# Partial sums kept in the token order of a head group, and another order of work in the first pair of a seven-product projection

## The chip, the cores and the metric

The kernel runs on one core of one Trainium2 chip. The metric is the device time of one execution in microseconds (us). Three executions of the kernel before took 2134.4, 2132.32 and 2133.94 us, so the median is 2133.94 us. One more execution was profiled: it took 2131.81 us, with a span of 2130.1 us from its first to its last instruction.

The engines are named as in the profile: PE is TensorE (matrix products), PEld its weight loads, DVE is VectorE, ACT is ScalarE, POOL is GpSimd, SP is SyncE, which here issues most of the transfers.

## The reference, cut to what matters

Two layers run over 1024 tokens of 1024 channels. The first mixes tokens with a gated position mixer, the second with dilated attention; each is followed by a dense squared-ReLU block. The change lies in the projection in front of the attention:

```python
WINDOW_DILATIONS = ((128, 1), (512, 4), (2048, 16))     # head groups g = 0, 1, 2
qkv = (h @ w_qkv).reshape(B_, S_, 3, N_DIL_GROUPS, ATT_HEADS, HEAD_DIM)
...
# in group g, query t attends to keys t - j*dilation, j = 0 .. window//dilation
s = einsum('bnqrhc,bnkrhc->bnrhqk', qb, kc) * HEAD_DIM ** -0.5
p = exp(logits - m); den = sum(p); num = einsum('bnrhqk,bnkrhc->bnqrhc', p, vc)
```

With dilation 4 or 16 the tokens that attend to each other are 4 or 16 apart. The kernel therefore keeps Q, K and V of group 1 and group 2 in another token order: all tokens of residue 0 first, then residue 1, and so on (`r q` in the code), while a projection comes out of PE in plain token order (`q r`). Group 0 has plain order in both.

## The kernel before, in words

**Units and pairs.** The attention is cut into 12 units, one for each pair of heads `hp` (4) and head group `g`, taken in the order of groups 1, 2, 0. Unit 0 is (hp 0, group 1), unit 1 is (hp 0, group 2), unit 2 is (hp 0, group 0), unit 3 is (hp 1, group 1), and so on. Each unit needs three tiles of 128 output channels by 1024 tokens: m = 0 is Q, m = 1 is K, m = 2 is V. The 36 tiles are projected two at a time. The first four tiles (Q, K and V of unit 0, and Q of unit 1) are done by the plain method (`classical`); the other 32 are 16 pairs, listed in `quads`. The pairs are made by `seven` (L1207 ff.).

**Seven products in place of eight.** A pair is a 2x2 block product (two tiles by two halves of 512 tokens). `one(p)` issues one of seven products: 4 blocks of 3 matmuls each, 12 matmuls of 128x512, into a bank of PSUM. There are three such banks (`mm`). `copied` (L1219, ACT) moves one product from PSUM to SBUF, `plus` (L1225, DVE) adds another product to a sum in SBUF, and `put_out` makes the four finished blocks: block (i, s) is tile i of the pair, token half s. Between products `more()` splits the weights of the next pair into a high and a low part (L205 on ACT, L206 on DVE), after some subtractions on POOL (L410 to L415).

**Where the order of tokens is changed.** `out_v` (V, L1144) and `out_qk` (Q and K, L1189) add the last product to the sum and write the result in the group's order. The inputs are read in plain order and the output is written with a stride. For Q and K ACT then writes the high part (L1192) and DVE the low part (L1193). A V block is transposed on PE and split (L1132 on ACT, L1133 on DVE). A block that is a single product has no addition: ACT (L1142 for V, L1192 for Q and K) and DVE (L1193) read it straight from PSUM, in the group's order.

**The attention beside it.** `attention` is a generator that is advanced between products. For each unit there are four rounds j: `scores` (PE matmuls into the `at` banks, then DVE adds the bias and takes a minimum, L1288, and ACT takes the exponential, L1290), `turned` (PE transposes, L187; ACT and DVE split the result, L205 and L206 with the tile name `tr`) and `values` (PE matmuls of `tr` with V; ACT copies the sum, L1327). The place of each step on PE is set by a count of PE time that the program keeps while it is written down (`Flow`): a step is put after the product at which its due time has passed. PE keeps exactly this order; on the other engines a scheduler decides the order when the program is built.

One rule cuts across this. When the first block of a K tile is put out, the program first runs the attention until all four score rounds of the unit before it are on PE:

```python
if m == 1 and i > 0:
    flow.until(lambda: U[i - 1].scored.t is not None)
u.tiles[m] = [slot((P, S), F32R, f"{'qk'[m]}{e}") for e in range(2)]
```

What `flow.until` has to bring forward stands on PE without products in between.

**The first pair.** For the first pair (`first=True`) the order of products is 1, 3, 6, 2, 7, 5, 4, since the terms for the products 4 and 5 are formed last. Tile 0 of this pair is K of unit 1, tile 1 is V of unit 1. The first block that is put out is (0, 0), after product 2.

Of the kernel before, what the change touches and what calls it, by code (L numbers as in the profile page):

```python
# [112 lines left out]
def trunk(ctx: ExitStack, tc: tile.TileContext, xT, w_u, w_v, w_o, w_s, b_s, w_qkv, w_bo, rel,  # L113
# [14 lines left out]
    def temp():  # L128
        return tpool.tile([P, HALF], F32, tag="t", name="t", bufs=NT)
# [950 lines left out]
    def permuted(t, s, g):  # L1080
# [4 lines left out]
        n = HALF // d  # L1085
        return t.rearrange("p (r q) -> p q r", r=d)[:, s * n:(s + 1) * n, :]

    def runs(t, g):
        return t if g == 0 else t.rearrange("p (q r) -> p r q", r=DIL[g])

# [7 lines left out]
    def own(t, g):  # L1098
        return t if g == 0 else t.rearrange("p (q r) -> p q r", r=DIL[g])
# [39 lines left out]
    def put(dst, a, b):  # L1139

        if b is None:
            nc.scalar.activation(dst, a, AF.Copy)  # L1142
        else:
            nc.vector.tensor_tensor(dst, a, b, op=ALU.add)  # L1144

    def out_v(i, s, a, b):

        u = U[i]
        ready = []
        with tc.high_priority(offset=PRIO):  # L1150
            if u.g < 2:
                t = temp()
                if u.g == 1 and b is None:
                    put(t.rearrange("p (r q) -> p r q", r=4), runs(a, 1), None)
                else:
                    put(t if u.g == 0 else t.rearrange("p (r q) -> p q r", r=4), own(a, u.g),
                        None if b is None else own(b, u.g))
                ready.append((s, t))
            else:
                for e in range(2):  # L1160
                    if e not in u.vt:
                        u.vt[e] = temp()
                    c = slice(8 * e, 8 * e + 8)
                    if b is None:
                        put(u.vt[e].rearrange("p (r q) -> p r q", r=8)[:, :, 32 * s:32 * s + 32], runs(a, 2)[:, c, :], None)
                    else:
                        put(u.vt[e].rearrange("p (r q) -> p q r", r=8)[:, 32 * s:32 * s + 32, :], own(a, 2)[:, :, c],
                            own(b, 2)[:, :, c])
                u.out += 1
                if u.out == 2:  # L1170
                    ready = [(e, u.vt.pop(e)) for e in range(2)]
        for part, t in ready:
            flow.add(v_side(i, t, part), LAT["ve"] + (500 if b is None else 1500) + (5000 if i == 0 else 0))

    def out_qk(i, m, s, a, b, over):

        u = U[i]
        if m not in u.tiles:
# [3 lines that stand above are left out]
        hi, lo = (runs_at(t, s, u.g) for t in u.tiles[m])  # L1182
        sc = -0.125 if m == 0 else 1.0
        with tc.high_priority(offset=PRIO):
            if b is None:
                a = runs(a, u.g)
            else:
                t = a if over and u.g == 0 else temp()
                nc.vector.tensor_tensor(t if u.g == 0 else t.rearrange("p (r q) -> p q r", r=DIL[u.g]),  # L1189
                                        own(a, u.g), own(b, u.g), op=ALU.add)  # L1190
                a = t if u.g == 0 else t.rearrange("p (r q) -> p r q", r=DIL[u.g])
            nc.scalar.activation(hi, a, AF.Copy, scale=sc)  # L1192
            nc.vector.scalar_tensor_tensor(lo, a, sc, hi.bitcast(F32), op0=ALU.mult, op1=ALU.subtract)  # L1193
        u.out_qk = getattr(u, "out_qk", 0) + 1
        if u.out_qk == 4:
            u.q, u.k = u.tiles[0], u.tiles[1]
            u.qk.t = flow.t

    def out(tile, s, a, b=None, over=False):

        i, m = tile
        if m == 2:
            out_v(i, s, a, b)
        else:
            out_qk(i, m, s, a, b, over)

    def seven(w, x, more, put_out, begun=None, first=False):  # L1207

        def one(p, bank=None):
            new = bank is None  # L1210
            bank = mm_bank() if new else bank
            product(bank, w[p], x.t[p], p in (2, 3, 4) and not (first and p == 3))
            more()
            return bank

        def copied(src):
            t = temp()
            with tc.high_priority(offset=PRIO):
                nc.scalar.activation(t, src, AF.Copy)  # L1219
            return t  # L1220

        def plus(x, y, out=None):
            out = temp() if out is None else out
            with tc.high_priority(offset=PRIO):
                nc.vector.tensor_tensor(out, x, y, op=ALU.add)  # L1225
            return out

        if first:
            a = one(1)
            u = copied(a)  # L1230
            d = one(3)
            plus(u, one(6), u)
            one(2, a)
            put_out(0, 0, a)
            e = one(7)
            c22 = plus(u, e)
            f = one(5)
            put_out(1, 1, c22, f, True)
            put_out(0, 1, plus(u, f), d, True)
        else:  # L1240
            u = one(6)
            if begun:
                begun()
            u = copied(u)
            a = one(1)
            plus(u, a, u)
            d = one(5)
            c22 = plus(u, d)
            e = one(7)
            put_out(1, 1, c22, e, True)  # L1250
            one(2, a)
            put_out(0, 0, a)
            one(3, d)
            put_out(0, 1, u, d)
        one(4, e)
        put_out(1, 0, u, e, True)

    def geometry(g, j):

# [265 lines left out]
    def ahead_of_last():  # L1525

        N = [slot(name="N") for _ in range(3)]
        for hp in range(3):
            nc.sync.dma_start(N[hp], kept_N[hp])
        yield 4000  # L1530
        for hp in range(3):
            for i in range(2):
                split_N(hp, i, N[hp][:, half(i)])
                yield 900
            proj_load(hp)
            yield 900
        proj_load(3)
        for k in range(KT):
            h[k] = slot(name=f"h{k}")
            nc.sync.dma_start(h[k], hd[k])  # L1540

    quads = [((1, 1), (1, 2))]
    for i in range(2, NU, 2):
        quads += [((i, 1), (i, 0)), ((i, 2), (i + 1, 0)), ((i + 1, 1), (i + 1, 2))]

# [17 lines left out]
    for n, two in enumerate(quads):  # L1563
        wn = Weights(qkv(*quads[n + 1])) if n + 1 < len(quads) else None
        more = ahead(wn)
        more()
        for i, m in two:
            if m == 1:
                U[i].bias = bias_tile(U[i].hp, U[i].g)
        seven(w, xa, more, lambda i, *x: out(two[i], *x), None if wn else lambda: flow.add(ahead_of_last()), n == 0)  # L1570
        w = wn
    half_done.t = flow.t

# [114 lines left out]
```

## Time and profile before

| What | Value |
|---|---|
| Time, median of 3 | 2133.94 us (2132.32 to 2134.4) |
| Profiled execution: its time, its span | 2131.81 us, 2130.1 us |
| PE busy | 2100.7 us, 99% of the span |
| DVE busy | 1598.3 us, 75% |
| ACT busy | 1102.5 us, 52% |
| POOL busy | 556.8 us, 26% |
| Granted TensorE clock | 0.998 of full speed |
| `plus` in the attention stage (L1225) | 31 times between 1000 and 1430 us, 685 ns each |
| Last addition of Q and K (L1189) | 31 times, 677 to 1131 ns, 938 ns in the mean |
| Last addition of V (L1144) | 128x512 forms: 11 times, 862 ns; 128x256 forms: 12 times, 632 ns |

The 16 pairs stand between 975 and 1425 us of the span, and the attention runs in the same stretch. A busy share is an average over the whole kernel. To see what a local change can be worth, read where PE itself stops: PE's timeline gives the start of each run of equal instructions and their count, so the stretch between two starts, less what the same instructions take where nothing holds them, is time in which PE waited.

### The profile page before, as it was taken

What the parts mean: (1) busy time and instruction counts of PE and PEld (TensorE: products, weight loads), DVE (VectorE), ACT (ScalarE), POOL (GpSimd) and SP (SyncE); (2) the same over time, 40 slices, a digit from 0 to 9 for tenths busy, and PEclk for the clock granted to TensorE, in tenths of its full rate; (3) what the DMA queues carried; (4) which work ended last, traced back from release to release, by engine and by line L of the source; (5) the groups of instructions that cost most, each with busy time, mean ns of one, the idle gap of its engine ahead of it and who ended that gap; (6) DMA issues with size and microseconds to landing.
All of it is one profiled execution on the core that took longest, in us unless ns stands there. A gap on an engine that the chain in (4) does not pass through costs nothing.

```text
span 2130.1 us, 30439 instructions
## 1 busy us (share of the span) xinstructions
PE 2100.7 (99%) x10426; PEld 1740.4 (82%) x10426; DVE 1598.3 (75%) x2918; ACT 1102.5 (52%) x2262; POOL 556.8 (26%) x417
## 2 busy tenths in 40 slices
PE   8999999999999999999999999999999999999998
PEld 7888887888878888887888788887888887888887
DVE  7975258576689888888776867778876667988886
ACT  7644136554574444346665656665555556544443
POOL 2100213223323322531212122101133332332345
PEclk9999999999999999999999999999999999999999
DMA  6411114455354444311112121141155544544432
GB/s 223 144 60 50 40 42 137 159 182 191 128 180 165 161 145 134 113 79 52 46 46 54 34 57 41 47 160 54 60 178 180 191 149 139 186 163 140 140 107 80
DMA packets 158815, 247.07 MB, mean 116 GB/s; under 512 B 33481, under 2 KB 47940, under 8 KB 158660
## 3 DMA queue, kind: packets, MB, share of 16 engines
q1 hardware_dynamic: 158336, 244.94, 35.1%
q8 instruction: 82, 1.34, 0.3%
q14 instruction: 73, 0.60, 0.1%
q10 hardware_dynamic: 324, 0.18, 0.0%
HBM read 180.41 MB, written 64.66 MB: 115 GB/s over the span
## 4 chain that ended last, share of the span: by engine, by line
PE 89%; DVE 6%; ACT 2%; issue 1%; DMA 1%; SPq 0%; DVEq 0%; ACTq 0%
PE at L180 44%; PE mm L180 43%; PE at L187 2%; DVE wp L206 1%; DMA t<-hid 1%; DVE t L206 1%; ACT t L1290 1%; DVE h L340 0%; DVE h L940 0%; ACT wp L205 0%; SPq L169 0%; DVE hx L206 0%; DVE raws L498 0%; DVE y L206 0%; DMA h<-hd 0%
## 5 line engine op out<-in xcount | busy, mean ns | idle before, releaser
L205 ACT ACTIVATE wp<-r 128x512 fp32r<-128x512 f32 (+3 forms) x490 | 294.9, 606 | 462.6 <-PE at L180 287.4
L180 PE MATMUL at<-hx,wp 128*128 128x512 f32 x1770 | 413.8, 389 | 5.0 <-DVE wp L206 3.2
L206 DVE TENSOR_TENSOR wp<-r,wp 128x512 fp32r<-128x512 f32 (+3 forms) x490 | 374.3, 768 | 36.9 <-ACT wp L205 33.2
L180 PE MATMUL mm<-y,wp 128*128 128x512 f32 x1608 | 396.5, 392 | 1.1 <-ACT t L1219 0.5
L180 PEld LDWEIGHTS at<-hx,wp 128*128 128x128 f32 x1770 | 331.8, 188 | 76.3 <-DVE wp L206 4.1
L180 PEld LDWEIGHTS mm<-y,wp 128*128 128x128 f32 x1608 | 298.5, 188 | 65.9 <-DVE h L340 1.6
L180 PE MATMUL at<-t,wp 128*128 128x512 f32 x1344 | 314.0, 389 | 0.1
L180 PEld LDWEIGHTS at<-t,wp 128*128 128x128 f32 x1344 | 252.2, 188 | 52.8 <-DVE t L803 0.5
L410 POOL TENSOR_TENSOR t<-r 128x512 f32<-128x512 f32 (+3 forms) x78 | 111.4, 1428 | 678.1 <-DMA r<-in_w_dn 270.4
L412 POOL TENSOR_TENSOR r<-r 128x512 f32<-128x512 f32 (+3 forms) x77 | 111.8, 1452 | 377.8 <-DVE wp L206 345.1
L180 PE MATMUL mm<-t,wp 128*128 128x512 f32 x768 | 191.5, 396 | 0.0
L206 DVE TENSOR_TENSOR hx<-t,hx 128x512 fp32r<-128x512 f32 x192 | 181.5, 958 | 5.4 <-ACT hx L205 5.3
L180 PE MATMUL mm<-hx,wp 128*128 128x512 f32 x708 | 171.8, 389 | 0.0
L180 PEld LDWEIGHTS mm<-t,wp 128*128 128x128 f32 x768 | 140.5, 188 | 29.6 <-DVE t L1225 0.3
L269 POOL TENSOR_TENSOR t<-t 128x512 f32<-128x512 f32 (+1 forms) x54 | 71.7, 1328 | 347.5 <-ACT t L258 345.6
L180 PE MATMUL mm<-y,whi 128*128 128x512 f32 x512 | 158.3, 390 | 0.0
L180 PEld LDWEIGHTS mm<-hx,wp 128*128 128x128 f32 x708 | 132.7, 188 | 28.0 <-DVE b L966 0.5
L940 DVE TENSOR_TENSOR h<-h,at 128x512 f32<-128x512 f32 x144 | 97.8, 681 | 55.3 <-PE at L180 55.3
L803 DVE TENSOR_TENSOR t<-t,at 128x512 f32<-128x512 f32 x116 | 79.2, 684 | 78.1 <-PE at L180 77.9
L180 PE MATMUL at<-y,wp 128*128 128x512 f32 x552 | 137.5, 390 | 0.0
L205 ACT ACTIVATE hx<-t 128x512 fp32r<-128x512 f32 x192 | 118.0, 628 | 30.2 <-DMA t<-hid 26.2
L415 POOL TENSOR_TENSOR r<-r 128x512 f32<-128x512 f32 (+3 forms) x77 | 105.3, 1367 | 85.6 <-issue 52.7
(224 smaller groups left out, 3120.7 us busy)
## 6 DMA issues: line engine op xcount, KB each, us to landing
t<-hid SPq DMA_DIRECT2D x194, 256.0 KB, 5.0
hid<-t SPq DMA_DIRECT2D x140, 256.0 KB, 2.3
r<-in_w_up SPq DMA_DIRECT2D x128, 256.0 KB, 2.8
r<-in_w_dn SPq DMA_DIRECT2D x88, 256.0 KB, 2.7
r<-in_w_qkv SPq DMA_DIRECT2D x72, 256.0 KB, 2.7
hid<-b SPq DMA_DIRECT2D x56, 256.0 KB, 2.8
r<-in_w_v SPq DMA_DIRECT2D x48, 256.0 KB, 3.5
h<-in_xT SPq DMA_DIRECT2D x16, 256.0 KB, 3.0
```

Of the source, the lines that this page charges most:

```text
L180: nc.tensor.matmul(out, lhsT, rhs, **kw)
L187: nc.tensor.transpose(out, src, ident)
L205: nc.scalar.activation(hi, src, AF.Copy)
L206: nc.vector.tensor_tensor(lo, src, hi.bitcast(F32), op=ALU.subtract)
L269: nc.gpsimd.tensor_tensor(self.acc, self.acc, sq, op=ALU.add)
L410: tt(r7, r[0, 0], r[1, 0], op=ALU.subtract)
L412: tt(r6, r[1, 0], r[0, 0], op=ALU.subtract)
L415: tt(r3, r[0, 1], r6, op=ALU.subtract)
L803: nc.vector.tensor_tensor(out, x, y, op=ALU.add)
L940: engine.tensor_tensor(hs[i, s], hs[i, s], src, op=ALU.add)
L1290: nc.scalar.activation(p[:, c], p[:, c], AF.Exp, bias=m, scale=-1.0, accum_out=dn)
```

## The change

Four things are changed, and nothing in the arithmetic.

1. `order_of` gives each pair a token order: that of its head group, where both tiles have the same group; where one tile has group 0, the order of the second tile's group; else plain order.
2. `copied` and `plus` keep the partial sums in this order. They read the product in PSUM with a stride (`runs`) and write SBUF without one.
3. In `out_v` and `out_qk`, where the tile's group is the pair's, the last addition is made the same way: the sum is read as it is stored, the product in PSUM with a stride, and the output is written without one. Where a tile of group 0 stands in a pair of another order, its V is put back into plain order by a strided read. Where the pair has plain order and the tile another (two pairs), it stays as before.
4. In the first pair V of unit 1 is tile 0 and K of unit 1 is tile 1. Block (1, 1), K's second half, is no longer put out after product 5. The sum for it is finished in place (`plus(c22, f, c22)`) and is put out after product 4, behind block (1, 0).

```diff
+    def order_of(two):
+        a, b = (U[i].g for i, _ in two)
+        return b if a == b or 0 in (a, b) else 0
+    def stored(t, g):
+        return t if g == 0 else t.rearrange("p (r q) -> p r q", r=DIL[g])
+    def unrolled(t, g):
+        return t.rearrange("p (q r) -> p q r", r=DIL[g])
...
     def out_v(i, s, a, b, go):
...
-                if u.g == 1 and b is None:
-                    put(t.rearrange("p (r q) -> p r q", r=4), runs(a, 1), None)
+                if b is None:
+                    put(stored(t, u.g), runs(a, u.g), None)
+                elif go == u.g:
+                    put(stored(t, go), stored(a, go), runs(b, go))
+                elif u.g == 0:
+                    put(unrolled(t, go), a.rearrange("p (r q) -> p q r", r=DIL[go]), unrolled(b, go))
                 else:
-                    put(t if u.g == 0 else t.rearrange("p (r q) -> p q r", r=4), own(a, u.g),
-                        None if b is None else own(b, u.g))
+                    put(t.rearrange("p (r q) -> p q r", r=4), own(a, u.g), own(b, u.g))
...
     def out_qk(i, m, s, a, b, over, go):
...
             if b is None:
-                a = runs(a, u.g)
+                a = stored(a, go) if over else runs(a, u.g)
             else:
-                t = a if over and u.g == 0 else temp()
-                nc.vector.tensor_tensor(t if u.g == 0 else t.rearrange("p (r q) -> p q r", r=DIL[u.g]),
-                                        own(a, u.g), own(b, u.g), op=ALU.add)
-                a = t if u.g == 0 else t.rearrange("p (r q) -> p r q", r=DIL[u.g])
+                t = a if over and u.g == go else temp()
+                if u.g == go:
+                    nc.vector.tensor_tensor(stored(t, go), stored(a, go), runs(b, go), op=ALU.add)
+                else:
+                    nc.vector.tensor_tensor(t.rearrange("p (r q) -> p q r", r=DIL[u.g]), own(a, u.g), own(b, u.g), op=ALU.add)
+                a = stored(t, u.g)
...
         def copied(src):
...
-                nc.scalar.activation(t, src, AF.Copy)
+                nc.scalar.activation(stored(t, go), runs(src, go), AF.Copy)
...
         def plus(x, y, out=None):
...
-                nc.vector.tensor_tensor(out, x, y, op=ALU.add)
+                nc.vector.tensor_tensor(stored(out, go), stored(x, go), runs(y, go), op=ALU.add)
...
         if first:
...
             c22 = plus(u, e)
             f = one(5)
-            put_out(1, 1, c22, f, True)
+            plus(c22, f, c22)
             put_out(0, 1, plus(u, f), d, True)
...
         one(4, e)
         put_out(1, 0, u, e, True)
+        if first:
+            put_out(1, 1, c22, None, True)
...
-    quads = [((1, 1), (1, 2))]
+    quads = [((1, 2), (1, 1))]
```

PE's order differs in one stretch only, from the second score round of unit 0 to the last score round of unit 1. In what follows `k_8538` and `k_8539` are the two parts of K of unit 0, `k_9069` and `k_9070` (before) and `k_9124` and `k_9125` (in the change) those of unit 1. Rows `mm<-t` and `mm<-y` are products, three matmuls to a row or a multiple of three, `at<-k,q` scores, `at<-ident,t` transposes, and `at<-tr,V` values.

The first place is PE in the first pair, behind the second score round of unit 0. Before:

```order
L180 MATMUL at<-k_8538,q_8535 128x256 x2
L180 MATMUL at<-tr,V 64x256 x3
L180 MATMUL at<-tr,V 64x128 x3
L180 MATMUL at<-tr,V 64x256 x3
L180 MATMUL at<-tr,V 64x128 x3
L187 MATMUL at<-ident,t 128x128 x6
L180 MATMUL at<-k_8538,q_8534 128x128 x2
L180 MATMUL at<-k_8539,q_8534 128x128 x2
L180 MATMUL at<-k_8538,q_8535 128x128 x2
L180 MATMUL at<-k_8538,q_8534 128x256 x2
L180 MATMUL at<-k_8539,q_8534 128x256 x2
L180 MATMUL at<-k_8538,q_8535 128x256 x2
```

Now:

```order
L180 MATMUL at<-k_8538,q_8535 128x256 x2
L180 MATMUL mm<-t_8729,wp 128x512 x3
L180 MATMUL mm<-t_8742,wp 128x512 x3
L180 MATMUL mm<-t_8764,wp 128x512 x3
L180 MATMUL mm<-t_8767,wp 128x512 x3
L180 MATMUL mm<-t_8770,wp 128x512 x3
L180 MATMUL mm<-t_8773,wp 128x512 x3
L180 MATMUL mm<-t_8776,wp 128x512 x3
L180 MATMUL at<-tr,V 64x256 x3
L180 MATMUL at<-tr,V 64x128 x3
L180 MATMUL at<-tr,V 64x256 x3
L180 MATMUL at<-tr,V 64x128 x3
```

Before, values, transposes and scores of two rounds followed each other with no product between; now 21 product matmuls stand ahead of the first of these rounds, 15 ahead of the second, and 21 ahead of the next values.

The second place is PE in the second pair, from the last block of its product 7. Tile 0 of that pair is K of unit 2, so its first block is held until the scores of unit 1 are on PE. Before:

```order
L180 MATMUL mm<-t_8767,wp 128x512 x3
L180 MATMUL mm<-y,wp 128x512 x12
L180 MATMUL at<-tr,V 64x128 x12
L187 MATMUL at<-ident,t 128x128 x4
L180 MATMUL at<-k_9069,q_8544 128x128 x2
L180 MATMUL at<-k_9070,q_8544 128x128 x2
L180 MATMUL at<-k_9069,q_8545 128x128 x2
L180 MATMUL at<-k_9069,q_8544 128x128 x2
L180 MATMUL at<-k_9070,q_8544 128x128 x2
L180 MATMUL at<-k_9069,q_8545 128x128 x2
L180 MATMUL mm<-y,wp 128x512 x12
```

Now:

```order
L180 MATMUL mm<-y,wp 128x512 x12
L180 MATMUL at<-tr,V 64x128 x12
L187 MATMUL at<-ident,t 128x128 x4
L180 MATMUL at<-k_9124,q_8544 128x128 x2
L180 MATMUL at<-k_9125,q_8544 128x128 x2
L180 MATMUL at<-k_9124,q_8545 128x128 x2
L180 MATMUL at<-k_9124,q_8544 128x128 x2
L180 MATMUL at<-k_9125,q_8544 128x128 x2
L180 MATMUL at<-k_9124,q_8545 128x128 x2
L180 MATMUL at<-tr,V 64x128 x12
L187 MATMUL at<-ident,t 128x128 x4
L180 MATMUL at<-k_9124,q_8544 128x128 x2
```

One round without products stood here before, now there are two, the second directly behind the first.

The third place is ACT late in the first pair, around K's first finished block (the row `k_9124<-t`), in the change. `t,st` are the exponentials of unit 0's third score round, the 128x128 and 128x256 parts of its two heads:

```order
L1309 ACTIVATE t,st_8854<-t,st_8854 128x128
L1309 ACTIVATE t,st_8854<-t,st_8854 128x256
L1309 ACTIVATE t,st_8854<-t,st_8854 128x128
L205 ACTIVATE wp<-r 128x512
L1209 ACTIVATE k_9124<-t 128x16x32
L1309 ACTIVATE t,st_8854<-t,st_8854 128x256
```

Before, the same four exponentials stood together, with none of K's blocks between them:

```order
L1290 ACTIVATE t,st_8854<-t,st_8854 128x128
L1290 ACTIVATE t,st_8854<-t,st_8854 128x256
L1290 ACTIVATE t,st_8854<-t,st_8854 128x128
L1290 ACTIVATE t,st_8854<-t,st_8854 128x256
L1327 ACTIVATE N<-at 64x256 x2
```

The last exponential of this round now stands behind K's high part, which waits for the last product of the pair.

More of the change, by code (lines that the diff above doesn't have):

```diff
@@ L1144, in put, with out_v @@
             nc.vector.tensor_tensor(dst, a, b, op=ALU.add)
-    def out_v(i, s, a, b):
+    def out_v(i, s, a, b, go):
         u = U[i]
@@ L1163, in out_v @@
                     c = slice(8 * e, 8 * e + 8)
-                    if b is None:
-                        put(u.vt[e].rearrange("p (r q) -> p r q", r=8)[:, :, 32 * s:32 * s + 32], runs(a, 2)[:, c, :], None)
+                    if b is None or go == 2:
+                        put(u.vt[e].rearrange("p (r q) -> p r q", r=8)[:, :, 32 * s:32 * s + 32],
+                            (runs if b is None else stored)(a, 2)[:, c, :], None if b is None else runs(b, 2)[:, c, :])
                     else:
@@ L1173, in out_v, with out_qk @@
             flow.add(v_side(i, t, part), LAT["ve"] + (500 if b is None else 1500) + (5000 if i == 0 else 0))
-    def out_qk(i, m, s, a, b, over):
+    def out_qk(i, m, s, a, b, over, go):
         u = U[i]
@@ L1197, in out_qk, with out, seven @@
             u.qk.t = flow.t
-    def out(tile, s, a, b=None, over=False):
+    def out(tile, s, a, b=None, over=False, go=0):
         i, m = tile
         if m == 2:
-            out_v(i, s, a, b)
+            out_v(i, s, a, b, go)
         else:
-            out_qk(i, m, s, a, b, over)
-    def seven(w, x, more, put_out, begun=None, first=False):
+            out_qk(i, m, s, a, b, over, go)
+    def seven(w, x, more, put_out, begun=None, first=False, go=0):
         def one(p, bank=None):
@@ L1569, in trunk @@
                 U[i].bias = bias_tile(U[i].hp, U[i].g)
-        seven(w, xa, more, lambda i, *x: out(two[i], *x), None if wn else lambda: flow.add(ahead_of_last()), n == 0)
+        seven(w, xa, more, lambda i, s, a, b=None, over=False: out(two[i], s, a, b, over, order_of(two)), None if wn else lambda: flow.add(ahead_of_last()), n == 0, order_of(two))
         w = wn
```

## The prediction

> **What bounds the kernel now.** I read the page first, then busy time by stretch, then PE's timeline where the order changes.
>
> ```profile
> span 2130.1 us, 30439 instructions
> PE 2100.7 (99%) x10426; PEld 1740.4 (82%) x10426; DVE 1598.3 (75%) x2918; ACT 1102.5 (52%) x2262; POOL 556.8 (26%) x417
> ...
> PE 89%; DVE 6%; ACT 2%; issue 1%; DMA 1%; SPq 0%; DVEq 0%; ACTq 0%
> ```
>
> PE bounds the span: 2100.7 of 2130.1 us. The change leaves every matmul in place, so a gain can only come from time in which PE stands still, and a loss only from new time of that kind. An addition on DVE that gets shorter is worth nothing unless PE waits behind it.
>
> ```profile
> 985.07:995.12 10.05, 7.77 (x62) 5.16 (x60) 5.28 (x23) 7.33 (x26) 0.00 (x0) 1.00 0.24 78
> 995.12:1029.50 34.38, 34.29 (x227) 28.61 (x226) 22.95 (x67) 20.50 (x63) 5.18 (x4) 1.00 0.16 41
> 1029.50:1186.00 156.50, 155.84 (x984) 130.46 (x983) 112.80 (x298) 92.71 (x256) 32.99 (x24) 1.00 0.18 48
> 1186.00:1220.00 34.00, 31.70 (x231) 26.62 (x229) 28.56 (x66) 21.50 (x57) 5.96 (x4) 1.00 0.09 32
> ```
>
> The columns are the stretch, its length, and busy PE, PEld, DVE, ACT and POOL. Where the change can act, PE is visibly idle in two places: 985 to 995 us, the two rounds without products in the first pair, and 1186 to 1220 us. Over the 156 us between them PE lacks 0.66 us. So the prize is a few us in 2130. A busy PE also hides waits between two matmuls, so I price the first place by starts and counts.
>
> **The change part by part.** First what it removes. The two rounds of unit 0 on PE:
>
> ```profile
> 983.40 0.82 PE L187 MATMUL at<-ident,t 128*128 128x128 f32 x6
> 984.15 0.96 PE L180 MATMUL at<-k,q 64*128 64x128 f32 x12
> 985.07 0.33 PE L180 MATMUL at<-tr,V 128*64 128x256 f32 x1
> ...
> 990.32 0.33 PE L180 MATMUL at<-tr,V 128*64 128x256 f32 x1
> ...
> 995.12 5.05 PE L180 MATMUL mm<-t,wp 128*128 128x512 f32 x21
> 1000.01 1.22 PE L180 MATMUL at<-tr,V 128*64 128x256 f32 x12
> 1001.07 0.84 PE L187 MATMUL at<-ident,t 128*128 128x128 f32 x6
> ```
>
> From start to start, 12 values take 1.06 us where nothing holds them (1000.01 to 1001.07), six transposes 0.75 (983.40 to 984.15), 12 scores 0.92 (984.15 to 985.07). A round is 2.73 us. The two rounds take 5.25 us (985.07 to 990.32) and 4.80 us (990.32 to 995.12), so PE waits 2.52 + 2.07 = **4.6 us**. In the change 21 products at 4.89 / 21 = 0.233 us (995.12 to 1000.01) stand ahead of the first round and 15 ahead of the second: 4.9 and 3.5 us of cover for waits of 2.5 and 2.1. I take all 4.6 us as removed.
>
> Now what it adds. One: product 5 of the first pair. There are three `mm` banks, and product 5 needs the one in which V's first block lies. V's block goes out by two ACT copies, and in ACT's order they stand behind the first exponential of a score round.
>
> ```profile
> 987.15 0.40 ACT L1290 ACTIVATE t<-t,st 128x128 f32<-128x128 f32 x1 [1.76 <-DVE st L1288]
> L1142 ACT ACTIVATE t<-mm 128x256 f32<-128x256 f32 x4 | 1.3, 383 | 2.5 <-PE mm L180 2.5
> ```
>
> That exponential, whose inputs don't change, ends at 987.55; the copies overlap by about 0.1 (4 take 1.3 us busy), so the bank is free at about 988.2. PE reaches product 5 after the 12 matmuls of product 7 from 985.2, at 988.0. A wait of 0.2, with handing over **0.3** (0 to 0.6).
>
> Two: the third place of the order. Two of six transposes of unit 0's third round wait for an exponential that now stands behind K's high part, which waits for the addition behind the pair's last product.
>
> ```profile
> L1225 DVE TENSOR_TENSOR t<-t,mm 128x512 f32<-128x512 f32 x31 | 21.2, 685 | 11.6 <-PE mm L180 11.4
> 1006.77 0.63 ACT L1192 ACTIVATE k<-t 128x512 fp32r<-128x512 f32 x1 [0.77 <-DVE t L1189]
> 987.55 0.49 ACT L1290 ACTIVATE t<-t,st 128x256 f32<-128x256 f32 x1
> ```
>
> From the last product's end: 0.69 + 0.63 + 0.49 = 1.8 us, and some 0.4 of handing over. PE covers 12 values and four transposes, 1.06 + 0.5 = 1.5 us. New wait: **0.7**. It is 0 if ACT's parts overlap more, and 1.1 if DVE comes to the addition 0.4 late, since two V halves and a weight split stand ahead of it. Behind the waiting transposes stand only that round's scores and the next products.
>
> Three: the second pair. K of unit 2 needs the scores of unit 1, which now start later, so one more round stands without products.
>
> ```profile
> 1025.90 0.88 PE L180 MATMUL at<-tr,V 128*64 128x128 f32 x12
> 1026.62 0.62 PE L187 MATMUL at<-ident,t 128*128 128x128 f32 x4
> 1027.17 0.89 PE L180 MATMUL at<-k,q 64*128 64x128 f32 x12
> 1027.99 3.02 PE L180 MATMUL mm<-y,wp 128*128 128x512 f32 x12
> ...
> 994.49 0.87 ACT L205 ACTIVATE tr<-at 128x384 fp32r<-128x384 f32 x2
> 995.01 1.02 DVE L206 TENSOR_TENSOR tr<-at,tr 128x384 fp32r<-128x384 f32 x2 [2.26 <-ACT tr L205]
> 1014.79 0.64 ACT L205 ACTIVATE tr<-at 128x256 fp32r<-128x256 f32 x2
> 1015.62 0.74 DVE L206 TENSOR_TENSOR tr<-at,tr 128x256 fp32r<-128x256 f32 x2
> ```
>
> Before, that one round (1025.90 to 1027.99) ran in 2.09 us with no wait, since its inputs came from scores long past. In the change the first of two rounds keeps this property; the second depends on transposes and scores of the first. It resembles the second of the removed rounds, which waited 2.07 us. It is narrower (256 against 384 columns): ACT's part of the split is 0.23 us shorter, DVE's 0.28. I take 2.07 - 0.5 = **1.5** (0 to 2.5, the longer of the two removed waits). V of unit 1 is transposed 18 products (4.2 us) before it is needed, so I cost its split at nothing.
>
> Four: small things. Both halves of unit 1's K now follow the pair's last product, a chain of 0.69 + 2 x 0.63 + 2 x 0.69 = 3.3 us; its first scores stand 21 products (4.9 us) and most of a round behind, so I cost it at nothing; if DVE or ACT came over 3 us late, PE would wait for the difference. On SP a load of weights and one of bias rows move ahead of the exchange of unit 0's sums (`sc`, `ex`); the loads only come earlier, and the exchange is read first in unit 2, a whole unit behind: nothing. Shuffled changes between kinds of matmul: 0.2 (-0.3 to 0.5).
>
> Five: the additions.
>
> ```profile
> 1005.64 1.10 DVE L1189 TENSOR_TENSOR t<-t,mm 128x512 f32<-128x512 f32 x1
> 1023.94 0.68 DVE L1189 TENSOR_TENSOR t<-t,mm 128x512 f32<-128x512 f32 x1
> L1189 DVE TENSOR_TENSOR t<-t,mm 128x512 f32<-128x512 f32 x31 | 29.1, 938 | 6.7 <-PE mm L180 6.5 <-PE at L187 0.2
> 947.45 0.68 DVE L1193 SCALAR_TENSOR_TENSOR k<-mm,k 128x512 fp32r<-128x512 f32 x1
> 948.70 0.69 DVE L1193 SCALAR_TENSOR_TENSOR q<-at,q 128x512 fp32r<-128x512 f32 x1
> ```
>
> Writing with a stride costs 1.10 against 0.68 us (group 2 at 1005.64, group 0 at 1023.94). With a mean of 0.938 some 19 of the 31 pay it; two still will. The new reads with a stride from PSUM have a near row: at 947.45 and 948.70 DVE reads K of group 1 and Q of group 2 from PSUM with strides of 4 and 16 elements, in 0.68 and 0.69 us. So I price them at the plain 0.69. DVE loses some 17 x 0.41 = 7 us, and a little in V, nearly all beside a busy PE. [...]
>
> Of this saving PE sees what lies on a chain that it waits for, at 1186 to 1220 us:
>
> ```profile
> 1202.67 1.26 DVE L1433 TENSOR_TENSOR dn<-f,st 128x8 f32<-128x8 f32 x1
> 1202.13 1.78 POOL L410 TENSOR_TENSOR t<-r 128x512 f32<-128x512 f32 x1 [22.75 <-PE at L187]
> 1208.39 1.02 DVE L1189 TENSOR_TENSOR t<-t,mm 128x512 f32<-128x512 f32 x1
> 1210.13 0.44 PE L180 MATMUL at<-k,q 64*128 64x128 f32 x4 [1.15 <-ACT q L1192]
> ```
>
> The addition at 1208.39 leads to Q's high part and so to PE's wait of 1.15 us: 1.02 - 0.69 = **0.3** gained. An earlier addition in this stretch also gets shorter, but an operation of 8 elements takes 1.26 us while POOL's of 1202.13 runs, which PE released; DVE would only reach that block earlier and wait it out. [...]
>
> The sum: -4.6 + 0.3 + 0.7 + 1.5 + 0.2 - 0.3 = **-2.2 us**. Against the profiled execution (2131.81 us, 1.7 around its span) that is 2129.6; against the median of 2133.94, from which that execution lies 2.1 down, it is **2131.7 us**.
>
> **The rivals.** The wait vanishes and nothing takes its place. For it: every new wait reaches down to 0 in my bounds, and each is a few tenths of chained handing over. Against: the second round's dependence is direct, and the like rounds both waited over 2 us. It gives -4.6 - 0.3 = -4.9, 2129.0 us.
>
> The wait moves and grows. Holding K to the end makes unit 1 late, and both bare rounds of the second pair wait as the first pair's did: 2.5 + 2.1 = 4.6, with 0.3, 1.1 and 0.2 beside them 6.2 new against 4.6 and 0.3 removed: +1.3, 2135.2 us, slower than before. It decides as soon as new waits pass 4.9 us. For it: both bare rounds are of the kind that waited. Against: the first one's inputs are four us old when PE comes to it.
>
> The change doesn't do what it says: reading PSUM with a stride costs DVE what writing with one did. Then the last additions stay at 1.1 and 20 sums (four in the first pair, two each in eight others) rise by 0.41: 8.2 us more on DVE. If five of them fall on something PE waits for, 2.0 us, and the 0.3 is lost: +0.1, 2134.0 us; with all exposed, 2140.2. Against it stand the rows at 947.45 and 948.70.
>
> **How the numbers follow.** Chances: the forecast 0.58, nothing in its place 0.20, grows 0.12, strided reads cost 0.10. A change within 0.2% (4.3 us) can't be told from none on this kernel. Faster by more comes from the second case, which lies just past that bound (0.15 of its 0.20), and the tail of the first (0.03): 0.18. Slower by more needs over 6 us against my sum: 0.03 from the growing wait, 0.03 from strided reads, 0.06. Within: 0.76. The range goes from the second case to the third, with a few tenths for the scatter of the three runs (2132.32 to 2134.4): 2128.8 to 2135.2.
>
> **What would show it.** Right: between the second score round of unit 0 and the end of the first pair PE has no stop but some tenths at product 5 and at most 1.1 us at the transposes behind it; in the second pair a stop of 1 to 2 us between the two bare rounds; the additions at 0.69 us with only two at 1.1; DVE's busy time down by 7 to 10 us; PE busy nearly as before. Wrong: no stop in the second pair (second case), stops over 4.9 us in all (third), `plus` at 1.1 us in pairs of groups 1 and 2 (fourth). A move at places behind 1430 us, where nothing changes, would say that I priced the wrong stretch.

## The result, and the profile after

The changed kernel takes 2129.14 us (median of 21 executions, 2127.34 to 2134.61), the kernel before, run beside it, 2134.39 us (2130.98 to 2136.77). The ratio is 0.9980, 95% interval 0.9973 to 0.9986: 4.3 us faster, with 3.0 to 5.8 as the bounds. The two medians differ by 5.3 us; here and below a gain is read from the recorded ratio. The forecast was 2131.7 us, 2.2 us faster. The direction and the range held; the gain is twice the sum.

The profiled execution of the changed kernel took 2131.43 us. The page's span, busy times and the shares of the chain of work that ended last:

```profile
span 2129.7 us, 30432 instructions
PE 2102.5 (99%) x10426; PEld 1743.5 (82%) x10426; DVE 1589.2 (75%) x2917; ACT 1104.5 (52%) x2264; POOL 560.1 (26%) x417
...
PE 90%; DVE 5%; ACT 2%; issue 1%; DMA 1%; DVEq 0%; SPq 0%; ACTq 0%
```

PE is the bound as before. DVE lost 9.1 us of busy time (1598.3 to 1589.2), inside the 7 to 10 that were forecast. The span is only 0.4 us shorter than that of the profiled execution before, so single profiles don't give the result; they show where PE stands. PE's timeline in the first pair, behind unit 0's second score round:

```profile
986.01 3.02 PE L180 MATMUL mm<-t,wp 128*128 128x512 f32 x12
989.19 2.34 PE L180 MATMUL mm<-t,wp 128*128 128x512 f32 x9 [0.16 <-ACT t L1153]
991.37 1.21 PE L180 MATMUL at<-tr,V 128*64 128x256 f32 x12
...
994.08 3.70 PE L180 MATMUL mm<-t,wp 128*128 128x512 f32 x15
997.62 1.22 PE L180 MATMUL at<-tr,V 128*64 128x256 f32 x12
...
1000.32 3.06 PE L180 MATMUL mm<-t,wp 128*128 128x512 f32 x12
```

The two rounds that waited now run in 2.71 us (991.37 to 994.08) and 2.70 us (997.62 to 1000.32), which is a round that nothing holds. One bracket is left: product 5 waits for the bank that V's block leaves by ACT's copies. In the second pair:

```profile
1020.42 0.88 PE L180 MATMUL at<-tr,V 128*64 128x128 f32 x12
1021.14 0.62 PE L187 MATMUL at<-ident,t 128*128 128x128 f32 x4
1021.69 0.89 PE L180 MATMUL at<-k,q 64*128 64x128 f32 x12
1022.57 0.27 PE L180 MATMUL at<-tr,V 128*64 128x128 f32 x1
1023.03 0.87 PE L180 MATMUL at<-tr,V 128*64 128x128 f32 x11 [0.19 <-DVE tr L206]
1024.15 1.48 PE L187 MATMUL at<-ident,t 128*128 128x128 f32 x4 [0.25 <-ACT t L1309]
1025.56 0.89 PE L180 MATMUL at<-k,q 64*128 64x128 f32 x12
1026.38 3.00 PE L180 MATMUL mm<-y,wp 128*128 128x512 f32 x12
```

The first of the two bare rounds takes 2.15 us (1020.42 to 1022.57), the second 3.81 us (1022.57 to 1026.38), where a round that nothing holds took 2.09 before. That is a stop of 1.7 us in small pieces; most of it is not in a bracket, because matmuls wait one by one for exponentials of 0.39 to 0.40 us each (four transposes take 1.41 us, 1024.15 to 1025.56, against 0.55).

At 1206 us, where a round's scores wait for a Q tile:

```profile
1204.36 1.61 PE L180 MATMUL at<-tr,V 128*64 128x128 f32 x18
...
1207.25 0.44 PE L180 MATMUL at<-k,q 64*128 64x128 f32 x4 [0.81 <-ACT q L1209]
1208.39 0.73 PE L180 MATMUL at<-k,q 64*128 64x128 f32 x8 [0.71 <-DVE q L1210]
```

The kernel before had three stops there. The first, at the values, is shown next and is gone; the one before Q's high part is 0.34 us shorter (1.15 in the row that the prediction shows, now 0.81); the third, 0.62 us before, is 0.71 now:

```profile
1206.95 1.57 PE L180 MATMUL at<-tr,V 128*64 128x128 f32 x17 [0.37 <-DVE tr L206]
```

The additions themselves, as DVE's groups by line, operation and shape in the changed kernel:

```profile
L1242 DVE TENSOR_TENSOR t<-t,mm 128x512 f32<-128x512 f32 x34 | 23.2, 684 | 11.6 <-PE mm L180 11.3
L1205 DVE TENSOR_TENSOR t<-t,mm 128x512 f32<-128x512 f32 x29 | 19.8, 683 | 5.4 <-PE mm L180 5.2
```

`plus` reads PSUM with strides of 4 and 16 elements now and takes 684 ns, where it took 685 with plain reads. So the rival "reading PSUM with a stride costs what writing with one did" is out: neither row shows a price of the strided reads. Why the strided writes of the kernel before took 1.10 us is not shown.

### The profile page after: what moved, and what is told of

The parts are those of the page before. It is cut to its first block, busy times and chain, and to the rows that moved or that the text cites. A ratio compares the mean times of both kernels' runs of the same rounds, so it can differ in the third digit from the quotient of the medians.

```text
span 2129.7 us, 30432 instructions
## 1 busy us (share of the span) xinstructions
PE 2102.5 (99%) x10426; PEld 1743.5 (82%) x10426; DVE 1589.2 (75%) x2917; ACT 1104.5 (52%) x2264; POOL 560.1 (26%) x417
## 3 DMA queue, kind: packets, MB, share of 16 engines
q8 instruction: 82, 1.34, 0.3%
## 4 chain that ended last, share of the span: by engine, by line
PE 90%; DVE 5%; ACT 2%; issue 1%; DMA 1%; DVEq 0%; SPq 0%; ACTq 0%
PE at L180 45%; PE mm L180 43%; PE at L187 2%; DVE wp L206 1%; DMA r<-in_w_up 1%; DVE t L206 1%; DVE h L340 0%; ACT wp L205 0%; DVE h L940 0%; DVE tr L206 0%; ACT t L1309 0%; DVE raws L498 0%; DVE y L206 0%; ACT t L205 0%; DVE t L1630 0%
```

## Experiments

Three theories were put to the chip first. **A**: the gain is PE's standing time, 2.6 us in the first two pairs by the new order and 0.8 us at 1206 us by the sums. **B**: it needs DVE's 9 us, so the sums carry it. **C**: a good part is scatter from short drops of the granted clock. Two more, **E** and **F**, belong to variants further down. To place a gain I use one more figure from the traces, "lost time": from each matmul's start to the next one's start, less the median of that for its kind (line and shape), summed over a stretch.

### The kernel before and the changed kernel once more

No edit.

> The kernel before, unchanged, as a control. Theory A (the gain is time in which PE no longer stands still): ratio 1.000 within 0.0005; PE's stretch from unit 0's second score round to the end of the second pair's two score rounds again 43.8 us, the waits near 1206 us again 2.7 us. Theory C (a good part of the measured gain is scatter from short drops of the granted clock): the control lies off 1 by more than 0.0005, or its runs scatter over 4 us or more, in step with their mean clock.

Measured: 2133.67 us, ratio 1.0003 (0.9994 to 1.0012). The first pairs and the waits at 1206 us came back (lost time in 985 to 1030 us: 6.75 and 6.61 us). These 11 runs scatter over 2.4 us, but the 33 of the same kernel beside them over 5.6 us, and those with a lower mean clock take longer (medians 2134.89 us at 0.996, 2133.36 at 0.997, 2133.13 at 0.998). So one of C's signs is there.

> The changed kernel once more. Theory A: -2.6 us in the first two pairs (43.8 to 41.2 us) and -0.8 us near 1206 us (2.7 to 1.9 us), less what the attention's end gives back, so -2 to -3.4 us, ratio 0.9984 to 0.9990. Theory C: the ratio moves by 0.0005 or more from the 0.998 measured first, either way, and the loss of 1.1 to 1.5 us at the attention's end does not come back.

Measured: 2128.29 us against 2133.41, ratio 0.9979 (0.9970 to 0.9988). The gain repeats at 4.5 us and is not scatter of the first comparison. It is also there between executions of equal mean clock: at 0.997 the changed kernel's median is 2129.65 us here and 2129.73 and 2129.98 in the two later comparisons, against 2133.36, 2134.28 and 2133.69 for the kernel before. So C falls as the cause. A's number, 2 to 3.4 us, is too small, so A lacks something.

### The order alone

The first pair of the change, with all sums in plain token order as before (the `go` of the change left out):

```diff
 # the kernel before, with
-            put_out(1, 1, c22, f, True)
+            plus(c22, f, c22)
...
+        if first:
+            put_out(1, 1, c22, None, True)
...
-    quads = [((1, 1), (1, 2))]
+    quads = [((1, 2), (1, 1))]
```

> The new order of the first pair alone (V first, K's second half held to the end); all partial sums stay in plain token order, so the strided writes at 1.1 us stay. PE's order is that of the changed kernel. Theory A: the whole -2.6 us of the first two pairs, nothing near 1206 us (2.7 us as before): ratio 0.9988. Rival B (the gain needs the 9 us that DVE loses): with the long additions back, the held K is late, the transposes of unit 0's third round wait 0.5 us or more, and under half of the 2.6 us comes: ratio 0.9994 or above.

Measured: 2130.14 us, ratio 0.9989 (0.9980 to 0.9998), 2.3 us faster. PE at 1206 us is as before, and the third round of unit 0 as in the changed kernel; product 5 waits a little longer (0.34 us, there 0.16):

```profile
989.08 2.34 PE L180 MATMUL mm<-t,wp 128*128 128x512 f32 x9 [0.34 <-ACT t L1142]
...
998.59 0.84 PE L187 MATMUL at<-ident,t 128*128 128x128 f32 x6
999.36 0.95 PE L180 MATMUL at<-k,q 64*128 64x128 f32 x12
...
1205.30 1.57 PE L180 MATMUL at<-tr,V 128*64 128x128 f32 x17 [0.35 <-DVE tr L206]
...
1208.49 0.44 PE L180 MATMUL at<-k,q 64*128 64x128 f32 x4 [1.16 <-ACT q L1192]
```

Theory A's number for this part holds. B's mechanism here (long additions make the held K late) does not show: the six transposes run in 0.77 us (998.59 to 999.36).

### The sums alone

The change with the old pair and nothing held:

```diff
 # the changed kernel, with
-            plus(c22, f, c22)
+            put_out(1, 1, c22, f, True)
...
-        if first:
-            put_out(1, 1, c22, None, True)
...
-    quads = [((1, 2), (1, 1))]
+    quads = [((1, 1), (1, 2))]
```

> The order of the partial sums alone; the first pair stays K, V and nothing is held, so PE's order is that of the kernel before. Theory A: the stretch of the first two pairs stays 43.8 us, the waits near 1206 us fall from 2.7 to 1.9 us, DVE's busy time falls by 8 to 9 us nearly all beside a busy PE: -0.8 us, ratio 0.9996. Rival B: half or more of the gain, -2 us or more, ratio 0.9990 or below, with the stretch of the first pairs shorter by 1 us or more.

Measured: 2131.41 us, ratio 0.9988 (0.9979 to 0.9997), 2.6 us faster. A expected 0.8, a ratio of 0.9996, which lies just inside the interval, so the time alone doesn't decide; the trace does. B had the size right, and its mechanism wrong: the first pairs still lose 6.44 us. The wait at 1206 us fell as A said; the rest lies where neither looked. Lost time by stretch, in us, one column for each profile (the last is four profiles of the changed kernel):

| Stretch | before, two | order alone | sums alone | changed, four |
|---|---|---|---|---|
| 985 to 1030 us, first two pairs | 6.75, 6.61 | 4.34 | 6.44 | 4.06, 4.04, 4.03, 4.20 |
| the waits at 1206 us | 2.68, 2.65 | 2.67 | 1.88 | 1.90, 1.89, 1.91, 1.89 |
| 1060 to 1190 and 1215 to 1400 us | 8.00, 7.91 | 8.47 | 6.77 | 6.68, 7.00, 6.70, 6.76 |
| 1400 to 1460 us, the attention's end | 2.02, 2.06 | 1.67 | 1.47 | 3.36, 2.88, 2.34, 2.42 |

The third row is what theory A lacked. Eight profiles fall into two groups by the sums, not by the order: about 8.1 without them, 6.8 with them (the variants below, all with the sums, lose 6.81, 7.52 and 6.98). The difference of 1.2 to 1.3 us lies in a handful of places where transposes or the scores behind them start 0.2 to 0.4 us late. One of them, first in the kernel before, then in the changed one:

```profile
1105.99 1.06 PE L187 MATMUL at<-ident,t 128*128 128x128 f32 x6
1106.98 0.33 PE L180 MATMUL at<-k,q 64*128 64x128 f32 x2
```

```profile
1104.14 0.84 PE L187 MATMUL at<-ident,t 128*128 128x128 f32 x6
1104.91 0.95 PE L180 MATMUL at<-k,q 64*128 64x128 f32 x12
```

Six transposes take 0.99 us, then 0.77. No bracket marks them; only starts against starts do. What the transposes wait for is the round's last exponential on ACT, again before, then now:

```profile
1105.95 0.51 ACT L1290 ACTIVATE t<-t,st 128x256 f32<-128x256 f32 x1 [0.39 <-DVE st L1288]
```

```profile
1103.48 0.51 ACT L1309 ACTIVATE t<-t,st 128x256 f32<-128x256 f32 x1 [0.39 <-DVE st L1307]
```

In the kernel before it ends at 1106.46, and the fifth transpose starts 0.15 us behind it, at 1106.61; in the changed kernel it ends at 1103.99, ahead of the first transpose. The other places were compared by lost time alone. **Theory A'**: the order gives 2.6, the sums 0.8 at 1206 us and 1.2 in small waits, and the attention's end gives back 0.7 in the mean. That makes 2.60 + 0.77 + 1.17 - 0.71 = 3.8 us, against 4.3, 4.5, 3.6 and 4.7 in the four comparisons of this study (the ratios 0.9980, 0.9979, 0.9983, 0.9978). The half us that is left is inside their intervals.

One thing is not in the table: the rest of 1190 to 1215 us, where a short drop of the granted clock falls (last section). It loses 1.45 to 1.49 us in the four profiles of the changed kernel and 1.50 with the sums alone, which all have the drop there; in the kernel before it loses 0.95 us with the drop, up to 1215 us, and nothing without, and with the order alone nothing. Counted in, these profiles would give 2.8 us. For executions that were not profiled the place of a drop isn't recorded, only the mean clock: 0.9972 over the four sets of the changed kernel, 0.9969 over the three of the kernel before beside it, which would be worth some 0.6 us in the changed kernel's favour (an estimate, 0.0003 of 2130 us). So the sum leaves the drops out.

### The changed kernel without the hold

```diff
 # the changed kernel, with
-            plus(c22, f, c22)
+            put_out(1, 1, c22, f, True)
...
-        if first:
-            put_out(1, 1, c22, None, True)
```

> The changed kernel without the hold: V is still the first tile of the first pair, but K's second half is put out as soon as its products are there. Since K's tile needs unit 0's scores done, the last two score rounds move up: 3 products instead of 15 stand ahead of unit 0's second round, and 12 products fall between other rounds. Theory A': the first round's wait (2.5 us) goes, the second's (2.1 us) keeps what 3 products of 0.233 us don't cover, 1.4 us: +1.0 to +1.4 us against the changed kernel, ratio to before 0.9984 to 0.9986. Rival: the hold only moves work and costs or saves under 0.3 us, ratio 0.998.

> The changed kernel a third time, beside its variants. Theory A': the gain is 2.6 us in the first two pairs plus some 2 us from the sums (0.8 at 1206 us, the rest in waits of 0.2 to 0.4 us between 1060 and 1360 us), -4.5 us, ratio 0.9979; the 1.2 to 1.7 us lost at the attention's end (1432 to 1460 us) comes back in this profile too if it belongs to the change. Rival: it is scatter of one transfer's landing; then this profile shows 0.8 to 1.3 us of waits there, as the kernel before does.

Measured, both on one chip: 2131.41 us (0.9991, 0.9982 to 1.0000) without the hold, 2129.83 us (0.9983, 0.9974 to 0.9992) with it, so the hold is worth 1.6 us, a little more than expected. The loss at the attention's end comes back smaller: from 1432 to 1460 us this third profile of the changed kernel loses 1.98 us, the first two 2.69 and 2.18, the kernel before 1.34 and 1.02. That it is more than before shows in each; how much of it is the change's own stays open. PE in the variant:

```profile
992.99 0.98 PE L180 MATMUL mm<-t,wp 128*128 128x512 f32 x3
993.80 1.22 PE L180 MATMUL at<-tr,V 128*64 128x256 f32 x12
...
997.06 0.44 PE L187 MATMUL at<-ident,t 128*128 128x128 f32 x2 [1.20 <-ACT t L1307]
...
998.31 3.06 PE L180 MATMUL mm<-t,wp 128*128 128x512 f32 x12
```

Three product matmuls stand ahead of the round in place of 15, and it takes 4.51 us (993.80 to 998.31) against 2.70: a stop of 1.8 us. V first alone takes one round's wait; the other goes only because the hold lets 12 more product matmuls pass ahead of it.

### The second pair treated like the first

Q first and K second in the second pair, K's second half held:

```diff
 # the changed kernel, with
-    def seven(w, x, more, put_out, begun=None, first=False, go=0):
+    def seven(w, x, more, put_out, begun=None, first=False, go=0, hold=False):
...
-            put_out(1, 1, c22, e, True)
+            if hold:
+                plus(c22, e, c22)
+            else:
+                put_out(1, 1, c22, e, True)
...
-        if first:
+        if first or hold:
             put_out(1, 1, c22, None, True)
...
-        quads += [((i, 1), (i, 0)), ((i, 2), (i + 1, 0)), ((i + 1, 1), (i + 1, 2))]
+        quads += [((i, 0), (i, 1)) if i == 2 else ((i, 1), (i, 0)), ((i, 2), (i + 1, 0)), ((i + 1, 1), (i + 1, 2))]
```

(`hold` is set for the second pair alone.)

> The changed kernel, and the second pair treated like the first: Q is the pair's first tile, K its second, and K's second half is held to the pair's end, so that 21 products stand ahead of the second score round that stood bare. Theory A': the stop of 1.8 us between 1022 and 1026 us goes, a wait of 0.3 us for a bank takes its place at most: -1.5 us against the changed kernel, ratio to before 0.9972. Rival E (the attention's end is bound by transfers): what PE gains ahead of it is waited for at the reload of h, waits at 1432 to 1460 us grow by 1 us or more, and the time stays that of the changed kernel.

Measured: 2127.20 us, ratio 0.9970 (0.9958 to 0.9981).

```profile
1021.44 3.02 PE L180 MATMUL mm<-y,wp 128*128 128x512 f32 x12
1024.29 2.20 PE L180 MATMUL mm<-t,wp 128*128 128x512 f32 x9
1026.33 0.88 PE L180 MATMUL at<-tr,V 128*64 128x128 f32 x12
...
1028.42 0.95 PE L180 MATMUL mm<-t,wp 128*128 128x512 f32 x3
```

The round behind the products takes 2.09 us (1026.33 to 1028.42): no stop is left. Lost time from 985 to 1030 us is 2.46 us against 4.08 in the mean of the changed kernel. At the attention's end it loses 1.83 us (2.42 in the repetition below), not more than the changed kernel, though PE comes there sooner, so rival E falls. Repeated on one chip with the changed kernel:

> The changed kernel beside the second-pair variant, on one chip. If the loss at the attention's end belongs to the change, this fourth profile again loses 0.8 us or more between 1400 and 1460 us against the 2.0 us that the kernel before loses there; if it is scatter of the reload's landing, it shows 2 us or less. If a step of the clock to half speed follows wherever PE was busy for half or less of the 3.41 us before, and never where it was busy for 0.6 or more, this profile has no exception.

> The second-pair variant once more, now with the changed kernel beside it on the same chip. The stop of 1.7 us between the second pair's score rounds is gone, so 1.6 us less than the changed kernel, up to 2.7 us if the first comparison's difference repeats; ratio to before 0.9970 to 0.9974. Rival: the first comparison was lucky, and the two are within 0.5 us.

Measured: 2129.89 us (0.9978, 0.9969 to 0.9987) and 2127.63 us (0.9971, 0.9959 to 0.9982). The changed kernel's fourth profile loses 2.42 us at the attention's end, between the two expectations; the clock's steps have no exception in it. The variant was faster than both kernels in both comparisons, by 2.6 and 2.3 us against the changed one in the medians, while the intervals of the ratios overlap. The stop that is gone is 1.6 of that; a likely part of the rest is told in the last section.

### K held in every later pair

```diff
 # the last variant, with
-        quads += [((i, 0), (i, 1)) if i == 2 else ((i, 1), (i, 0)), ((i, 2), (i + 1, 0)), ((i + 1, 1), (i + 1, 2))]
+        quads += [((i, 0), (i, 1)), ((i, 2), (i + 1, 0)), ((i + 1, 2), (i + 1, 1))]
```

(`hold` is set wherever K is the second tile.)

> As the last, with K second and held in every later pair that holds Q and K or K and V. PE waits in no bare round of those pairs, so theory A' expects no more than the second pair's 1.5 us from it: ratio 0.9970 to 0.9974. Rival F (a held K is late for the scores behind the pair's end, a chain of 3.3 us behind the last product): new waits of 1 to 2 us at the start of units 3 to 5, and the time at or above that of the changed kernel.

Measured: 2142.64 us, ratio 1.0044 (1.0032 to 1.0057), 6.8 to 12.2 us slower than the kernel before. It is slower, as F said, but not at the place that F named. Between 1030 and 1400 us the lost time is 1.7 us more than in the first profile of the changed kernel; from 1400 to 1460 us, behind the last pair, where no further products stand, it is 15.6 us against 3.4.

```profile
1419.31 0.84 PE L180 MATMUL mm<-t,wp 128*128 128x512 f32 x3
1424.60 1.90 PE L180 MATMUL at<-tr,V 128*64 128x128 f32 x12 [4.45 <-ACT tr L205]
...
1437.05 0.33 PE L180 MATMUL at<-k,q 64*128 64x128 f32 x2
1442.06 1.44 PE L180 MATMUL at<-k,q 64*128 64x128 f32 x10 [4.68 <-DVE k L1210]
```

PE stands 9.1 us in two stops, the first for a split on ACT, the second for the low part of the held K. ACT ahead of the first, and DVE ahead of the second:

```profile
1422.13 1.36 ACT L205 ACTIVATE wp<-r 128x512 fp32r<-128x512 f32 x2 [6.14 <-DMA r<-in_w_up]
```

```profile
1438.25 0.69 DVE L340 TENSOR_TENSOR h<-h,mm 128x512 f32<-128x512 f32 x1 [1.91 <-DMA h<-hd]
...
1440.72 1.28 DVE L1210 SCALAR_TENSOR_TENSOR k<-t,k 128x512 fp32r<-128x512 f32 x2
```

Both engines stand behind a transfer first: ACT waits 6.14 us for weights, and DVE 1.91 us for the reload of `h`, while K's high part has been ready since 1435.4 us. F's chain of 3.3 us behind the last product has no transfer in it, so its mechanism isn't shown; why the hold makes these two orders so costly stays open. The hold paid in the first and the second pair, where it took a stop away; held in every later pair, the lost time grew by 1.7 us up to 1400 us and by 12.2 us behind it.

## Why the prediction came out as it did

**The two rounds removed, -4.6 us: right.** Both run in the 2.7 us of an unheld round.

**Product 5's bank, +0.3: right.** The 12 products ahead of it take 3.18 us up to its start (986.01 to 989.19), where 12 at 0.233 take 2.80: 0.4.

**The transposes of the third round, +0.7: did not occur.** The failing step is "an exponential that now stands behind K's high part, which waits for the addition behind the pair's last product". ACT in the changed kernel:

```profile
997.00 0.62 ACT L1209 ACTIVATE k<-t 128x512 fp32r<-128x512 f32 x1
997.52 0.50 ACT L1309 ACTIVATE t<-t,st 128x256 f32<-128x256 f32 x1
...
999.16 0.64 ACT L1209 ACTIVATE k<-t 128x512 fp32r<-128x512 f32 x1 [0.53 <-DVE t L1205]
```

Two high parts of K stand here. The one ahead of the exponential is the held half's, whose last addition, behind product 5, ended by 996.9 us; it waits for nothing. The one that waits for the last product (L1205) stands behind the exponential. I read the order by the name of the tile and took one half for the other, there and in the section on the change, where the row `k_9124<-t` is the held half. The bound of 0 was in the text; the value chosen was 0.7.

**The second pair, +1.5: 1.7.** The stop stands between the two bare rounds, as forecast; the second-pair variant, in which it is gone, shows that it is that wait and what it is worth.

**The additions beside a busy PE, at nothing: the largest miss.** "An addition on DVE that gets shorter is worth nothing unless PE waits behind it" holds here: of the 9.1 us that DVE lost, PE's lost time shows 1.9 (0.77 + 1.17). But the next step, that outside 1186 to 1220 us PE doesn't wait, came from a row that shows 0.66 us idle in 156 us, and the prediction has no row behind 1220 us. Such small waits hardly appear as idle time: in the run of six shown above each transpose is drawn busy for 0.27 us and, unheld, the next one starts 0.11 us after it, so a start that comes 0.16 us late leaves no gap. They were worth 1.2 us, as the sums alone show.

**The addition at 1208 us, -0.3: -0.8.** The chained part measured 0.34. The other 0.5 is the stop at the values. Of the shorter addition ahead of it I said that DVE would "only reach that block earlier and wait it out", the block beside POOL's operation (an addition of 128x8 takes 1.26 us there, where the median of its line, L1433, is 0.16). It did not, because POOL's operation came earlier too:

```profile
1199.69 1.67 POOL L410 TENSOR_TENSOR t<-r 128x512 f32<-128x512 f32 x1 [22.31 <-PE at L187]
```

It starts 4.67 us ahead of the values here (1204.36) and 4.23 us ahead in the kernel before (1202.13 to 1206.36), in both within 0.1 us of the end of DVE's weight split that stands before it. All eight profiles with the new sums and K held in the second pair at most show 4.67 and no stop at the values, all three without them 4.23 and the stop.

**Behind 1430 us, nothing: +0.7.** The prediction named a move there as a sign of the wrong stretch. It moved, though it is small beside the rest. DVE waits for the reload of `h`, here in the changed kernel and in the kernel before:

```profile
1431.28 0.69 DVE L340 TENSOR_TENSOR h<-h,mm 128x512 f32<-128x512 f32 x1 [1.10 <-DMA h<-hd]
```

```profile
1432.32 0.69 DVE L340 TENSOR_TENSOR h<-h,mm 128x512 f32<-128x512 f32 x1 [0.27 <-DMA h<-hd]
```

The reload's eight transfers take 8.7 to 9.4 us from issue to landing (median of the eight) in four profiles of the changed kernel, 8.3 and 8.5 in two of the kernel before, 7.7 and 8.0 with one part alone. Either part alone loses nothing there. Why they land later with both stays open.

**Small things, +0.2: not seen.** The parts above make -2.5 us in the first two pairs, and the lost time there fell by 2.6.

So the sum, with what was measured: -4.6 + 0.4 + 0 + 1.7 - 0.8 - 1.2 + 0.7 = -3.8 us, against -2.2. The number of the rival "nothing takes its place" (2129.0 us) is next to the result, but its mechanism isn't the one: the second pair's stop was there, and what made up for it came from the sums. The range held with 0.3 us to spare at its lower end (2128.8). And the sentence that a change within 0.2% can't be told from none is wrong here: all four comparisons, at 0.9978 to 0.9983, have intervals that leave 1 out.

## What to carry to other kernels

Where dependent rounds stand bare on PE, find the rule that brings them forward; delaying the tile that triggers it, where later products can cover it, took the wait away here (lost time in the first two pairs: 6.7 us before, 4.1 in the changed kernel, 2.5 with the second pair treated like the first). In every pair, the last one included, the same delay cost far more than it gave (15.6 us of lost time at the attention's end against 3.4 in the changed kernel). A busy engine in the profile isn't proof that nothing waits: compare starts of equal runs of instructions (six transposes in 0.77 or 0.99 us) before a shorter operation beside them is priced at nothing. Where an order decides a term, follow which half of a tile each instruction handles, not its name.

## What the runs showed of the hardware

In these profiles the granted clock fell to 0.50 for one step of 3.41 us behind some stretches of that length in which PE stood about half the time. In the changed kernel, stretch by stretch (columns as in the prediction, the clock behind POOL):

```profile
1205.59:1209.00 3.41, 1.89 (x21) 1.44 (x19) 3.41 (x7) 1.79 (x4) 0.83 (x1) 1.00 0.01 2
1209.00:1212.41 3.41, 3.41 (x14) 2.77 (x11) 3.38 (x11) 1.54 (x6) 2.69 (x2) 0.50 0.20 77
```

PE was busy for 1.89 of 3.41 us, with no single wait over 1 us, and the next 3.41 us ran at 0.50. In the twelve profiles of this study, cut into such steps from the first one at full speed and the last microseconds of the program left aside, a half-speed step followed each step in which PE was busy for at most 0.49 of it, none in which it was busy for 0.58 or more, and six of the eleven between 0.53 and 0.56. The two long stops of the last variant do the same:

```profile
1419.35:1422.76 3.41, 0.80 (x4) 0.34 (x2) 0.00 (x0) 0.63 (x1) 0.00 (x0) 1.00 0.74 150
1422.76:1426.17 3.41, 1.49 (x11) 1.30 (x12) 2.14 (x4) 2.42 (x7) 0.00 (x0) 0.50 0.46 129
```

Two things follow. Such a step cost 1.2 to 1.6 us: from 1190 to 1215 us, which holds the same two waits, the changed kernel lost 3.35 to 3.40 us in its four profiles, all with a half-speed step there, and the three profiles of the variants, without one, 1.79 us (no hold), 2.18 and 1.76 us (second pair). In the kernel before, where the step reaches past 1215 us, 1190 to 1220 us lost 4.30 us with it and 3.00 without. And where a stop lies against the steps made a difference: in the two profiles of the second-pair variant the same waits fall across the border of two steps (busy 0.72 and 0.63 in the lower one), and no drop follows. That may be the rest of its gain over the changed kernel; it was not tried by itself. It also accounts for part of the scatter: in one set of 11 executions of the changed kernel those with a mean clock of 0.998 took 2127.0 to 2127.5 us, those with 0.997 took 2128.3 to 2130.4; in other sets the two groups overlap, so it isn't all of it.
